# A decoder step with retention, RWKV-7 and product-key experts: the last gathered tile's sums stay in PSUM, and the first tile's output projection stands beside the second projection group

## The chip, the core and the metric

The kernel runs on one core of a Trainium2 chip. The metric is the device time of one execution in microseconds. The engines are named as in the profile: PE (TensorE: matmuls and transposes), DVE (VectorE), ACT (ScalarE), POOL (GpSimd), and SP, whose queue issues most of the DMAs. Each engine takes its instructions in the order in which they stand in its own list, and each DMA queue likewise.

## What is computed

One layer for 1024 prompt tokens and 64 sample tokens, width 1024, all in float32. Cut to the main line:

```
xn   = rmsnorm(h) * g
proj = xn @ w_in                          # 2048 retention + 1792 RWKV columns
out  = concat(retention(proj), rwkv7(proj)) @ w_out
h    = h + out
xn   = rmsnorm(h) * g2                    # PEER: 128 x 128 experts, 8 heads, top 16 each
q    = xn @ wq ; scores against two key sets ; top-k of top-k -> 128 experts per token
y    = sum_k gelu(xn . u[e_k]) * softmax_k * v[e_k]
h    = h + y
gate = sigmoid(rmsnorm(h) * g3 @ ple_gate)
h    = h + gate * (p @ ple_proj)
out  = rmsnorm(h) * g4
```

The recurrent states are outputs too. The two parts that the change touches are `h = h + out` for the first 128 tokens, and `h = h + y` for one tile of 128 tokens.

## The kernel before

The tokens are nine tiles: 0 to 7 are the prompt's, 128 tokens each, and 8 holds the 64 sample tokens.

**Projection.** `group_a` multiplies by `w_in` in three groups of tiles, `A0` = 0 and 1, `A1` = 2 and 3 (group two), `A2` = 4 to 8 (group three). Each streams all of `w_in` from HBM, splits every weight in a high and a low part, and uses three matmuls for one (L332, L333, L335). `a_ret` makes the retention columns (`pret` in PSUM), `a_rw` the RWKV columns (`prw`).

**Mixers.** `mixers(t)` does retention and RWKV for tile t. Tile 0's runs interleaved with groups one and two; its output row `od0` goes to HBM in two halves (L522, L994). The others follow group three in `group_b`.

**Rows.** `c_rows(t)` is the output projection of a tile: it loads x (L594) and `od` (L599), transposes (L604), multiplies by `w_out`, streamed in 16 pieces (L620, L621), adds (L624), stores `hd` (the residual stream, L625), norms, and stores `xd` (the experts' input, L639). In before, tile 0's call stands in `build` behind group two, and every step of it is followed by one step of group three (L1487).

**Experts.** Five tiles fetch their experts' rows one by one. `early_query` loads `xd` (L1196) and the query weights (L1213), multiplies (L1220), and picks the experts. `gather` then makes 128 steps over `u` (64 for tile 8): POOL issues an indirect DMA that brings one expert's row per token (L1146), and DVE multiplies it by x and sums (L1160); then as many steps over `v`, where DVE adds the weighted row onto `gacc` (L1172 the first, L1174 the others). `gacc` is one tile of two PSUM banks with a single buffer, which holds first x (L1154) and then the sums, so the gathers of tiles 0, 1, 8 (`E0`, in `early`) and 2, 3 (`G1`) follow each other. At the end of a gather ACT copies the sums to SBUF (L1178) and stores them in HBM as `yd` (L1179). Tiles 4 to 7 (`G2`) go through all 16384 experts as dense matmuls (`dense_fused`, `dense_stored`), with `gates` ahead of that for their routing weights; tiles 2 and 3 gather beside it.

**Last stage.** `ple` takes the tiles in the order 0, 1, 8, 4, 5, 6, 7, 2, 3. For each it loads `hd`, adds the experts' sums (a load of `yd`, L1424, and an add, L1425; the dense tiles' by transposes, L1430 and L1431), norms and transposes (L317, L326), then for each half of the columns 24 matmuls with the gate's weights (`ppg`), a sigmoid (L1440, L1441), 6 matmuls with the projection (`ppp`), L1444 and L1445, and at last the norm and the store of the output (L1448 to L1454).

**What sets the order.** The program is recorded with generators that yield after each small step; `build` and `interleave` decide which generator is asked next. A scheduler of the framework then fixes each engine's list from that, with priorities in the order of recording and a timing model of its own. So moving one call moves instructions on every engine.

Of the kernel before, what the change touches and what calls it, by code (L numbers as in the profile page):

```python
# [14 lines left out]
OP = mybir.AluOpType  # L15
# [166 lines left out]
E0 = [0, 1, 8]  # L182
G1 = [2, 3]
# [7 lines left out]
IB = 2  # L191
# [4 lines left out]
G2 = [4, 5, 6, 7]  # L196
# [21 lines left out]
class K:  # L218
# [917 lines left out]
    def gather(self, gp, t, rows=("grow",), parts=1, acc=None):  # L1136


        nc, I = self.nc, self.I
        n = SIZE[t]  # L1140
        slot = lambda name, tag: gp.tile([128, D], F32, name=name, tag=tag, bufs=GBUF if len(rows) == 1 else 1 + (tag == "V"))
        home = lambda: acc.tile([128, 2, 512], F32, name="gacc", bufs=1).rearrange("p a b -> p (a b)")

        def fetch(src, j):
            g = slot("grow", rows[j % len(rows)])
            nc.gpsimd.indirect_dma_start(out=g, out_offset=None, in_=src,  # L1146
                                         in_offset=bass.IndirectOffsetOnAxis(ap=self.eid[t][:, j:j + 1], axis=0))
            return g

        x = slot("gx", rows[-1])  # L1150
        for k in range(0, 128, n):
            nc.sync.dma_start(x[k:k + n], self.xd[t][:n])
        xs, x = x, home()
        nc.scalar.activation(x, xs, AF.Copy)  # L1154
        hv = gp.tile([128, parts, 128], F32, name="hv")[:, :, :n]
        cs = [slice(i * D // parts, (i + 1) * D // parts) for i in range(parts)]
        for j in range(n):
            g = fetch(I['pu'], j)
            for i, c in enumerate(cs):
                nc.vector.scalar_tensor_tensor(g[:, c], g[:, c], 1.0, x[:, c], op0=OP.mult, op1=OP.mult, accum_out=hv[:, i, j:j + 1])  # L1160
            yield j
        ac = gp.tile([128, 128], F32, name="ac")[:, :n]
        for i in range(1, parts):
            nc.vector.tensor_tensor(hv[:, 0], hv[:, 0], hv[:, i], op=OP.add)
        nc.scalar.activation(ac, hv[:, 0], AF.Gelu)
        nc.vector.tensor_tensor(ac, ac, self.gsm[t], op=OP.mult)
        y = home()
        for j in range(n):
            g = fetch(I['pv'], j)
            for c in cs:  # L1170
                if j == 0:
                    nc.vector.tensor_scalar(y[:, c], g[:, c], ac[:, 0:1], None, op0=OP.mult)  # L1172
                else:
                    nc.vector.scalar_tensor_tensor(y[:, c], g[:, c], ac[:, j:j + 1], y[:, c], op0=OP.mult, op1=OP.add)  # L1174
            if j < n - 1:
                yield j
        ys, y = y, slot("gy", rows[-1])
        nc.scalar.activation(y, ys, AF.Copy)  # L1178
        nc.scalar.dma_start(self.yd[t], y)  # L1179
        yield n  # L1180
# [225 lines left out]
    def ple(self, rp, tps, yT):  # L1406
        nc, I, O = self.nc, self.I, self.O
# [3 lines left out]
        for i, t in enumerate(E0 + G2 + G1):  # L1411
            tp = tps[i % 2]
            n = SIZE[t]
# [4 lines left out]
            self.split(pth[:, :, :n], ptl[:, :, :n], pt[:, :, :n])  # L1418
            h = tps[0].tile([128, D], F32, name="ph", bufs=3)
            nc.sync.dma_start(h[:n], self.hd[t][:n])  # L1420
            if t not in G2:
                for k in range(0, 128, n):
                    y = tp.tile([128, D], F32, name="py", tag="njunk")
                    nc.sync.dma_start(y[:n], self.yd[t][k:k + n])  # L1424
                    nc.vector.tensor_tensor(h[:n], h[:n], y[:n], op=OP.add)  # L1425
            else:
                o = self.off[t]
                p = self.pst.tile([128, 2, 512], F32, name="pyt").rearrange("p c (a b) -> p (c a) b", b=128)
                for d in range(8):
                    nc.tensor.transpose(p[:n, d, :], yT[:, d, o:o + n], self.c("ident"))  # L1430
                nc.vector.tensor_tensor(h[:n].rearrange("p (a b) -> p a b", b=128), h[:n].rearrange("p (a b) -> p a b", b=128), p[:n], op=OP.add)  # L1431
# [24 lines left out]
    def build(self):  # L1456
        PS = bass.MemoryType.PSUM
        run = lambda g: [None for _ in g]
        sb = lambda name, es, **kw: self.pool(name, es=es, reuse_waits="tile", **kw)
        with self.es:  # L1460
            self.setup()
            em, ee, eg, et, ew, ex, ep, e0, e1, e2 = (ExitStack() for _ in range(10))
# [10 lines left out]
            a = self.group_a(pools, A0, "b", mixes)  # L1473
            while next(a) != "rw":
                pass
            m = mix[0]
            self.interleave(m, 1, a, IA)
            a = self.group_a(pools, A1, "b")
            self.interleave(m, IB, a, 1)
            e1.close()  # L1480
            e0.close()
            self.ep0 = ep0 = sb("early", ee, side="right")
# [1 line left out]
            early = self.behind(self.early(ep0), PE_)  # L1484
            co = self.co = sb("co", ew, side="right")
            a = self.group_a(self.a_pool(e2, "2"), A2, "b")
            for _ in self.c_rows(co, E0[0]):  # L1487
                next(a, None)
            for _ in a:
                for _ in range(IE):  # L1490
                    next(early, None)
# [52 lines left out]
            with ExitStack() as e:  # L1544
# [9 lines left out]
                for i, t in enumerate(G2 + [None]):  # L1554
                    tk = self.topk(tp, t) if t is not None else iter(())
                    while True:
                        a, b = next(tk, "end"), next(gate, "end")
# [43 lines left out]
```

## Time and profile before

| | us |
|---|---|
| three timed runs | 3719.7, 3698.1, 3711.76 (median 3711.76) |
| the profiled execution | 3716.76 |
| its span, from the first to the last instruction | 3714.7 |

The profile's tables are read so. A line `L1174 DVE ... x571 | 731.9, 1282 | ...` is a group of instructions: how many, their busy time in us, the mean of one in ns, the idle time of the engine ahead of them and what ended it. A windows row gives, for a stretch of time, its length, the busy time (and number) of each engine, the clock that TensorE was granted (1.00 is full), the share of time in which the DMA engines were busy, and their rate. A row of the chain of waits is a start, a duration and what the end of the program was waiting for then.

The gathers' landmarks, from the tile view of `gacc`: the first tile's x is copied in at 447.7 us, the last tile's at 2980.9; the first sums are copied out at 1151.4 and the last at 3676.2.

### The profile page before, as it was taken

How to read it: one execution, taken by the hardware profiler on the slowest of the kernel's cores; microseconds unless marked ns; L12 is line 12 of the kernel's file. 1: busy time of each engine (PE TensorE's matmuls, PEld its weight loads, DVE VectorE, ACT ScalarE, POOL GpSimd, SP SyncE). 2: the span in 40 equal slices, each digit the busy share in tenths (PEclk: the TensorE clock that was granted, in tenths of full speed). 3: DMA queues.
4: the chain of work that ended last, by engine and by line, in shares of the span. 5: the costliest groups of instructions: out<-in, count | busy, mean ns of one | idle time of the engine just before them, and what ended most of it. 6: DMA issues, size and time to landing. Idle time of an engine off the chain costs nothing. (4 is left out here: it accounts for less than half of the span.)

```text
span 3714.7 us, 52379 instructions
## 1 busy us (share of the span) xinstructions
PE 3304.0 (89%) x17749; PEld 2745.7 (74%) x17749; DVE 2846.8 (77%) x5655; ACT 1216.7 (33%) x2260; POOL 2338.1 (63%) x2068
## 2 busy tenths in 40 slices
PE   7799995868869978897999999999999998899996
PEld 7698994645747866675887878887888876677774
DVE  5544578878796698877997989766777777877886
ACT  4232220111112111112334877863332333333322
POOL 5354276455454455555468877768888878887752
PEclk9799995667868567788999999999999999999998
DMA  7266588889867888889679988999999999999974
GB/s 254 84 207 207 190 276 290 275 276 326 290 218 278 299 274 280 287 287 328 212 253 320 327 291 291 341 344 348 342 340 346 332 357 366 370 361 360 330 270 157
DMA packets 423846, 1075.74 MB, mean 290 GB/s; under 512 B 46299, under 2 KB 143321, under 8 KB 418906
## 3 DMA queue, kind: packets, MB, share of 16 engines
q0 software_dynamic: 165888, 604.05, 46.1%
q1 hardware_dynamic: 202814, 377.55, 30.4%
q10 hardware_dynamic: 54876, 90.79, 6.6%
q8 instruction: 141, 2.31, 0.2%
q14 instruction: 127, 1.04, 0.1%
HBM read 981.46 MB, written 90.70 MB: 289 GB/s over the span
## 5 line engine op out<-in xcount | busy, mean ns | idle before, releaser
L1146 POOL DMA_INDIRECT grow<-in_pv,eid x576 | 567.1, 985 | 476.8 <-DVE gacc L1174 249.6
L1146 POOL DMA_INDIRECT grow<-in_pu,eid x576 | 560.9, 974 | 403.5 <-DVE grow L1160 222.1
L1160 DVE SCALAR_TENSOR_TENSOR grow<-grow,gacc 128x1024 f32<-128x1024 f32 x576 | 692.2, 1213 | 138.0 <-DMA grow<-in_pu,eid 123.2
L1174 DVE SCALAR_TENSOR_TENSOR gacc<-grow,ac,gacc 128x1024 f32<-128x1024 f32 x571 | 731.9, 1282 | 54.9 <-DMA grow<-in_pv,eid 46.9
L1329 PE MATMUL py<-ah,vh 128*128 128x512 f32 x1024 | 406.0, 397 | 31.5 <-ACT vh L303 28.6
L332 PE MATMUL ph<-cx,uh 128*128 128x512 f32 x1024 | 406.6, 397 | 11.9 <-DVE al L305 7.5
L1330 PE MATMUL py<-al,vh 128*128 128x512 f32 x1024 | 404.5, 395 | 3.1 <-DVE al L305 3.1
L333 PE MATMUL ph<-cx,uh 128*128 128x512 f32 x1024 | 405.5, 396 | 0.0
L307 POOL TENSOR_TENSOR vl<-vraw,vh 128x640 fp32r<-128x640 f32 (+1 forms) x224 | 325.4, 1458 | 39.3 <-ACT vh L303 29.5
L307 POOL TENSOR_TENSOR ul<-uraw,uh 128x1024 fp32r<-128x1024 f32 x128 | 307.8, 2404 | 59.4 <-ACT uh L303 30.5
L1332 PE MATMUL py<-ah,vl 128*128 128x512 f32 x1024 | 271.2, 396 | 6.9 <-POOL vl L307 6.8
L335 PE MATMUL ph<-cx,ul 128*128 128x512 f32 x1024 | 268.3, 398 | 2.3 <-POOL ul L307 2.3
L1329 PEld LDWEIGHTS py<-ah,vh 128*128 128x128 f32 x1024 | 194.7, 190 | 83.1 <-ACT vh L303 37.4
L303 ACT ACTIVATE vh<-vraw 128x640 fp32r<-128x640 f32 (+1 forms) x224 | 154.4, 692 | 266.9 <-DMA vraw<-in_pvd 89.6
L332 PEld LDWEIGHTS ph<-cx,uh 128*128 128x128 f32 x1024 | 195.0, 190 | 52.7 <-DVE al L305 7.9
L1332 PEld LDWEIGHTS py<-ah,vl 128*128 128x128 f32 x1024 | 191.4, 189 | 56.0 <-POOL vl L307 15.4
L1336 DVE TENSOR_TENSOR yT<-yT,py 128x512 f32<-128x512 f32 x216 | 147.6, 685 | 105.7 <-PE py L1332 86.1
L1330 PEld LDWEIGHTS py<-al,vh 128*128 128x128 f32 x1024 | 195.0, 190 | 45.1 <-DVE al L305 4.8
L333 PEld LDWEIGHTS ph<-cx,uh 128*128 128x128 f32 x1024 | 194.8, 190 | 38.4
L335 PEld LDWEIGHTS ph<-cx,ul 128*128 128x128 f32 x1024 | 191.6, 190 | 41.5 <-POOL ul L307 4.0
L303 ACT ACTIVATE uh<-uraw 128x1024 fp32r<-128x1024 f32 x128 | 135.4, 1058 | 149.5 <-DMA uraw<-in_puT 95.3
L1273 DVE TENSOR_TENSOR oh<-csta,pit 128x1024 f32<-128x1024 f32 x128 | 153.7, 1213 | 28.9 <-PE pwt L1278 15.9
(401 smaller groups left out, 7305.9 us busy)
## 6 DMA issues: line engine op xcount, KB each, us to landing
uraw<-in_puT SPq DMA_DIRECT2D x128, 512.0 KB
vraw<-in_pvd SPq DMA_DIRECT2D x128, 320.0 KB
cw<-in_w_out SPq DMA_DIRECT2D x128, 256.0 KB
wd<-wst ACTq DMA_DIRECT2D x28, 1024.0 KB
wt<-wd SPq DMA_DIRECT2D x64, 448.0 KB
wraw<-in_w_ret SPq DMA_DIRECT2D x48, 512.0 KB
ewq<-in_wq SPq DMA_DIRECT2D x48, 512.0 KB
vraw<-in_pvd SPq DMA_DIRECT2D x96, 256.0 KB
```

The costliest lines, as they stand in the source:

```text
L303: nc.scalar.activation(hi, src, AF.Copy)
L307: nc.gpsimd.tensor_tensor(lo, src, hi.bitcast(F32), op=OP.subtract)
L332: mm(out, lh(k), rh(k), start=first and k == 0, stop=False)
L333: mm(out, *((ll(k), rh(k)) if right else (lh(k), rl(k))), start=False, stop=False)
L335: mm(out, *((lh(k), rl(k)) if right else (ll(k), rh(k))), start=False, stop=last and k == nk - 1)
L1146: nc.gpsimd.indirect_dma_start(out=g, out_offset=None, in_=src, in_offset=bass.IndirectOffsetOnAxis(ap=self.eid[t][:, j:j + 1], axis=0))
L1160: nc.vector.scalar_tensor_tensor(g[:, c], g[:, c], 1.0, x[:, c], op0=OP.mult, op1=OP.mult, accum_out=hv[:, i, j:j + 1])
L1174: nc.vector.scalar_tensor_tensor(y[:, c], g[:, c], ac[:, j:j + 1], y[:, c], op0=OP.mult, op1=OP.add)
L1273: nc.vector.tensor_tensor(oh, io, p[:, 0:2, s + b:s + b + 4, None].to_broadcast([128, 2, 4, 128]), op=OP.is_equal)
L1329: nc.tensor.matmul(p, vh[:, b, :], ah, start=b == 0, stop=False)
L1330: nc.tensor.matmul(p, vh[:, b, :], al, start=False, stop=False)
L1332: nc.tensor.matmul(p, vl[:, b, :], ah, start=False, stop=b == nb - 1)
```

## The change

The first edit ends the gather of the last tile, `G1[-1]` = 3, without the copy, the store and the slot for them. The sums stay in `gacc`, and `ple` adds them from there. The other gathered tiles go through HBM as before.

The second edit takes the call `c_rows(co, 0)` from its place behind group two and puts it behind tile 0's mixer in the generator `first`, which `interleave` runs beside group two: `IB` = 2 steps of it for one of the group. It gets buffers of its own, the pool `co0`, which closes with group two's pools. Group three is then recorded with the early work alone.

```diff
@@ gather
+        if t == G1[-1]:
+            self.sums = y
+            yield n
+            return
         ys, y = y, slot("gy", rows[-1])
         nc.scalar.activation(y, ys, AF.Copy)
         nc.scalar.dma_start(self.yd[t], y)
@@ ple
-            if t not in G2:
+            if t == G1[-1]:
+                nc.vector.tensor_tensor(h[:n], h[:n], self.sums, op=OP.add)
+            elif t not in G2:
                 for k in range(0, 128, n):
                     y = tp.tile([128, D], F32, name="py", tag="njunk")
                     nc.sync.dma_start(y[:n], self.yd[t][k:k + n])
@@ build
             a = self.group_a(pools, A1, "b")
-            self.interleave(m, IB, a, 1)
+            co0 = sb("co0", e1, side="right")
+
+            def first():
+                yield from m
+                yield from self.c_rows(co0, E0[0])
+
+            self.interleave(first(), IB, a, 1)
             e1.close()
             e0.close()
...
             a = self.group_a(self.a_pool(e2, "2"), A2, "b")
-            for _ in self.c_rows(co, E0[0]):
-                next(a, None)
             for _ in a:
                 for _ in range(IE):
                     next(early, None)
```

Behind the first edit the lines of the changed kernel have higher numbers: by 4 from `gather` on, by 6 behind the add in `ple`, by 10 at the end.

Three places in the engines' lists show the move. First, SP's queue in the second half of group two. Before: the group's last weights (L534) between the first loads of group three (L375, L357), and tile 0's projection (L594, L599, L620) behind all of them.

```order
L375 DMA wraw<-in_w_ret 128x1024
L534 DMA wraw<-in_w_rw 128x1024 x2
L375 DMA wraw<-in_w_ret 128x1024 x2
L357 DMA x<-in_x 128x1024 x2
L534 DMA wraw<-in_w_rw 128x1024
L375 DMA wraw<-in_w_ret 128x1024
L534 DMA wraw<-in_w_rw 128x1024 x2
L357 DMA x<-in_x 64x1024
L534 DMA wraw<-in_w_rw 128x1024
L594 DMA ch<-in_x 128x1024
L599 DMA cot<-od_92 128x512 x2
L620 DMA cw<-in_w_out 128x512 x2
```

Now, in the same half of the group, SP's list reads:

```order
L534 DMA wraw<-in_w_rw 128x1024 x7
L599 DMA cot<-od_92 128x512
L620 DMA cw<-in_w_out 128x512 x3
L534 DMA wraw<-in_w_rw 128x1024 x2
L620 DMA cw<-in_w_out 128x512 x2
L534 DMA wraw<-in_w_rw 128x1024
L620 DMA cw<-in_w_out 128x512 x2
L534 DMA wraw<-in_w_rw 128x1024
L620 DMA cw<-in_w_out 128x512 x3
L534 DMA wraw<-in_w_rw 128x1024
```

The pieces of `w_out` stand between the group's last seven weights, behind a load of `od0` that waits for tile 0's mixer, and group three's loads have moved behind them.

Second, SP's queue where tile 0's query begins (L1196 loads its `xd`, L1213 its weights). Before, that is deep in group three, behind the sample states of the mixers (L433):

```order
L433 DMA sr<-in_s_ret 64x512
L391 DMA rope<-in_rope 128x256 x2
L1196 DMA exn<-xd_83 128x1024
L1213 DMA ewq<-in_wq 128x1024 x3
L391 DMA rope<-in_rope 128x256
```

Now it stands at the group's head (L1200, L1215 and L1217 are the former L1196, L1211 and L1213):

```order
L244 DMA row_norm_mix<-in_rows 128x1024
L375 DMA wraw<-in_w_ret 128x1024 x2
L357 DMA x<-in_x 128x1024 x2
L391 DMA rope<-in_rope 128x256 x3
L375 DMA wraw<-in_w_ret 128x1024 x3
L357 DMA x<-in_x 128x1024 x2
L1200 DMA exn<-xd_83 128x1024
L1215 DMA ekT<-in_keysT 128x128
L1217 DMA ewq<-in_wq 128x1024
```

The query has moved ahead of most of the group's own loads.

Third, the end of DVE's list, from the last-but-one tile (2) on. Before, the last gather steps (L1174) stand behind tile 2's output (L1453), and tile 3's add (L1425) behind them:

```order
L1441 TENSOR_SCALAR psg<-psg 128x512
L1174 SCALAR_TENSOR_TENSOR gacc<-grow,ac,gacc 128x1024
L1444 TENSOR_TENSOR psg<-psg,ppp 128x512
L1174 SCALAR_TENSOR_TENSOR gacc<-grow,ac,gacc 128x1024
L1445 TENSOR_TENSOR ph<-ph,psg 128x512
L1174 SCALAR_TENSOR_TENSOR gacc<-grow,ac,gacc 128x1024 x2
L1453 SCALAR_TENSOR_TENSOR fin<-ph,frs,row_norm_final 128x512 x2
L1174 SCALAR_TENSOR_TENSOR gacc<-grow,ac,gacc 128x1024 x3
L1425 TENSOR_TENSOR ph<-ph,py 128x1024
L317 SCALAR_TENSOR_TENSOR njunk<-ph,nrs,row_ple_norm 128x1024
```

Now (L1426 is the new add, L1447, L1450, L1451 and L1459 the former L1441, L1444, L1445 and L1453) the same end of DVE's list is:

```order
L1174 SCALAR_TENSOR_TENSOR gacc<-grow,ac,gacc 128x1024
L1426 TENSOR_TENSOR ph<-ph,gacc 128x1024
L1447 TENSOR_SCALAR psg<-psg 128x512
L1459 SCALAR_TENSOR_TENSOR fin<-ph,frs,row_norm_final 128x512 x2
L1450 TENSOR_TENSOR psg<-psg,ppp 128x512
L317 SCALAR_TENSOR_TENSOR njunk<-ph,nrs,row_ple_norm 128x1024
L1451 TENSOR_TENSOR ph<-ph,psg 128x512
L1447 TENSOR_SCALAR psg<-psg 128x512
```

The last gather step and tile 3's add stand ahead of tile 2's first sigmoid (the upper L1447), and tile 3's norm (L317) between tile 2's halves.

## The prediction

> **What bounds the kernel now.** I read the page first, then the stages, then the end.
>
> ```profile
> span 3714.7 us, 52379 instructions
> PE 3304.0 (89%) x17749; PEld 2745.7 (74%) x17749; DVE 2846.8 (77%) x5655; ACT 1216.7 (33%) x2260; POOL 2338.1 (63%) x2068
> L1160 DVE SCALAR_TENSOR_TENSOR grow<-grow,gacc 128x1024 f32<-128x1024 f32 x576 | 692.2, 1213 | 138.0 <-DMA grow<-in_pu,eid 123.2
> L1154 ACT ACTIVATE gacc<-gx x5: 1009/1029/1122, 447.7 to 2980.9; 128x1024 f32<-128x1024 f32 x5
> ```
>
> No engine is full over the whole span. Two strands run beside each other. One is the matrix work on PE. The other is the gather: 1152 DVE steps (576 of L1160 and 576 of L1172 and L1174) in one PSUM tile `gacc`, so the five tiles follow each other. It begins at 447.7 us (the tile view's row of L1154) and, as the chain below shows, ends at 3676.2, close to the end of everything. Busy time of each engine in eight stages, from one answer of the windows view (columns: window, its length, PE, weight loads, DVE, ACT, POOL, granted clock, DMA share, GB/s):
>
> ```profile
> 253.00:303.00 50.00, 39.38 (x293) 37.72 (x291) 30.24 (x50) 20.13 (x31) 30.61 (x25) 0.90 0.74 255
> 303.00:577.00 274.00, 258.38 (x2010) 249.35 (x2009) 163.76 (x466) 66.53 (x146) 136.42 (x147) 0.97 0.71 237
> 577.00:1197.00 620.00, 484.58 (x2740) 365.44 (x2741) 501.95 (x943) 92.59 (x208) 311.13 (x309) 0.70 0.82 279
> 1740.00:1960.00 220.00, 216.62 (x1211) 187.99 (x1212) 207.68 (x938) 69.93 (x110) 134.85 (x107) 1.00 0.74 246
> 2400.00:3000.00 600.00, 592.51 (x2704) 493.01 (x2703) 445.12 (x613) 232.29 (x388) 490.56 (x394) 0.99 0.96 341
> 3000.00:3530.00 530.00, 488.42 (x2050) 385.98 (x2048) 426.81 (x697) 195.69 (x321) 421.61 (x352) 0.98 1.00 359
> 3530.00:3715.00 185.00, 142.32 (x636) 112.18 (x636) 140.15 (x170) 41.90 (x79) 73.77 (x85) 0.89 0.63 213
> ```
>
> The third projection group (303 to 577) and the first part of the dense stage (2400 to 3000) are PE's; from 3000 to 3530 the DMA engines are full as well. A gather step there lies beside other work. In the last window PE is busy for only 142 of 185 us, and the chain of waits says why:
>
> ```profile
> 3542.66 1.24 DVE ph L1425
> ...
> 3674.90 1.30 DVE gacc L1174
> 3676.22 1.03 ACT gy L1178
> 3677.28 2.63 DMA yd<-gy
> 3679.96 3.32 DMA py<-yd
> 3683.31 1.24 DVE ph L1425
> ...
> 3688.09 1.94 PE ntr L326 x8
> ...
> 3706.05 0.49 PE ppp L335 x2
> ...
> 3710.28 1.30 DVEq L1597
> ```
>
> The last tile's gather ends at 3676.2, its sums go to HBM and back, and only then does that tile's last stage run, alone. PE's own rows for the last three tiles (the end of each half of a tile is the ppp row):
>
> ```profile
> 3650.92 0.63 PE L335 MATMUL ppp<-pgb,ptl 128*128 128x512 f32 x2
> 3657.73 0.62 PE L335 MATMUL ppp<-pgb,ptl 128*128 128x512 f32 x2
> 3664.53 0.61 PE L335 MATMUL ppp<-pgb,ptl 128*128 128x512 f32 x2
> 3688.09 1.94 PE L326 MATMUL ntr<-csta,njunk 128*128 128x128 f32 x8 [22.94 <-DVE njunk L317]
> ```
>
> PE waited 22.94 us for the last tile. A half of a tile costs 3657.73 - 3650.92 = 6.8 us when PE is fed.
>
> **The change part by part. (1) The sums stay in PSUM.** Removed: the copy L1178 (1.03 us), its store (2.63) and its load (3.32); with the gaps between them the add moves from 3683.31 to 3676.2, 7.1 us. The add itself reads PSUM in place of SBUF; I cost that at nothing. What is late next is the gather itself, and that is moved by the other part.
>
> **(2) The gather's lead.** Counted in DVE's order of before, 1102 gather steps stand ahead of the second L1425 (the one at 3542.66); in the change's order 1113 do, 11 more. From there to the first-half sigmoid of tile 2 it is 40 steps in before and 39 in the change, so DVE carries the same load per tile, but it finishes the gather one tile earlier: the new add stands just ahead of that L1441, which in before ran here:
>
> ```profile
> 3657.66 0.43 DVE L1441 TENSOR_SCALAR psg<-psg 128x512 f32<-128x512 f32 x1 [0.62 <-ACT psg L1440]
> ```
>
> So tile 3's sums are ready while PE still works on tile 2, and tile 3's transposes follow PE's 3664.53 + 0.61 = 3665.1 directly. From there: transposes about 1 us, two halves at 6.8, so PE ends near 3679.8. Behind the last matmul the trace shows 3714.7 - 3706.5 = 8.2 us of sums, square, norm and store, which stay. New end 3688.0 at an unchanged start of the stage: **-26.7 us**. The 7.1 us of part 1 are inside it, not beside it. Without the lead they are all there is.
>
> **(3) The projection of tile 0 moved into group two.** What it issues: two loads of `od0`, one of x, 16 quarter-megabyte loads of W_out and two rows on SP's queue; 8 transposes and 32 matmuls on PE; the copies, sums and norm of one tile on ACT, DVE and POOL; two stores. The same instructions, some 50 us earlier. What it needs, and when it ran (rows of the timeline, of the window of L621 alone, of PE's waits from 253 to 311, of the tile view of `ewq`, and of the page's list of DMAs):
>
> ```profile
> 250.84 0.33 ACTq L994 DMA_DIRECT2D od<-hnx  x1
> ...
> 303.08 0.33 SPq L594 DMA_DIRECT2D ch<-in_x  x1
> ...
> 303.00:353.00 50.00, 15.54 (x32) 5.29 (x32) 0.97 0.61 187
> ...
> PE prw L332 <- ACT rb L552: 4.2, 1, 4.2
> ...
> 365.52 0.33 SPq L1196 DMA_DIRECT2D exn<-xd  x1
> L1213 SPq DMA_DIRECT2D ewq<-in_wq x16: 327/328/468, 365.9 to 421.1; - x16
> ...
> cw<-in_w_out SPq DMA_DIRECT2D x128, 256.0 KB
> ewq<-in_wq SPq DMA_DIRECT2D x48, 512.0 KB
> ```
>
> Tile 0's mixed rows are stored at 250.84, while group two still runs to 303. The projection there costs PE 15.54 us (the window of L621 alone), and before it lay in a stage where PE had 258 of 274 us. In 253 to 303 PE was idle for 50 - 39.38 = 10.6 us, one wait of them 4.2 us long for ACT. If the matmuls fill all of that, the two groups end 10.6 us earlier; if the 16 x 256 KB = 4.2 MB are not hidden on the DMA engines, which moved 255 GB/s there against 359 in the busiest stage, they cost 4.2 MB / 359 GB/s = 11.7 us. All six rows of PE's waits there name ACT, DVE or POOL (the longest is quoted) and none a load, so the filled end is the nearer one, and I take half the idle time: **-5 us** (ends -10.6 and +11.7).
>
> The clock belongs here. The granted clock was 0.90 in this window, against 1.00 in 1740 to 1960. The Trainium skill's page "TensorE: Matmul & The Clock Gate", section "HAM oscillation — how this bites in real kernels", says that idle gaps of PE over about 3.4 us send it back to half clock. The 4.2 us wait is such a gap, and the lower grant fits it. By the rule this term would go to its end of -10.6, if the moved matmuls close that gap; and the rule speaks against the change at the next place, if a new gap opens there.
>
> That next place is the head of group three. Tile 0's query now begins there at once: counted in PE's order, about 25 matmuls of the group stand ahead of it in place of some 360. Its 16 loads of half a megabyte were spread over 365.9 to 421.1 among the group's matmuls. At worst all 8.4 MB stand exposed at 359 GB/s: +23.4 us; at best nothing. SP's queue has been rearranged so that the first of them go out behind the group's fourth row tile, and PE still has the group's matmuls between the heads: **+2 us**.
>
> **(4) The mixers.** From 577 to 1740 DVE is the busiest engine (501.95 of 620 us in the first part). Between the first state update of the mixers and the last projected tile, before has 349 gather steps in DVE's order and the change 341. Eight steps at 1.213 us are 9.7 us; had DVE been the chain throughout, all of that would be won, were the gather hidden, none; a new order may also lose as much: **-3 us** (ends -10 and +10). In the query, gate and dense stages the counts of the two orders differ by at most three steps. No change there.
>
> The sum: -26.7 - 5 + 2 - 3 = **-32.7 us**. The profiled execution took 3716.76 us, 2.1 more than its span, and that is 5.0 above the median of the three runs shown (3711.76). 3716.76 - 32.7 = 3684.1; as a median 3711.76 - 32.7 = 3679.1.
>
> **The rivals.** *The lead is eaten.* The gather gains 11 places in DVE's order, but its rows come late (L1160 waited 123.2 us for them, above), so it ends as close to the end as before, and only the copy and two transfers go: 3711.8 - 7.1 = 3704.7. For it: DMA is full from 3000 to 3530. Against: the steps are pinned in order between instructions of the same tiles, at the density of before. *More is won.* Group two's idle time is filled to the last and the mixers give all of 9.7 us: -26.7 - 10.6 - 9.7 = -47.0, so 3664.8. For it: DVE's share in the mixers. Against: part of DVE's time there is a wait for others. *The weights of the early work come late* (the other side): group two waits 11.7 us for W_out, group three's head 23.4 us for the query's weights, the mixers lose 10 through the order, and since tile 0's experts are then known late, the gather's lead is gone too. That is -7.1 + 45.1 = +38.0, so 3749.8, slower. It is slower than before from the point where 7.1 of those 45.1 us are exposed, and by more than a measurement can miss from 25.7. Against it: PE did not wait for a load in this stretch, and DMA had a quarter of its time left (0.74 and 0.71). *The change does nothing*: it would need the old place of the last add; the order shows another.
>
> **How the numbers follow.** Forecast 3679, its own range 3665 to 3693: 0.52. More is won, around 3665 or below: 0.13. The lead is eaten, around 3705: 0.22. Late weights, 3712 to 3750: 0.13. About 0.5% (18.6 us) is what a measurement of this kernel can tell from no change, so faster means below 3693.2 and slower above 3730.3. Faster takes the first two cases, 0.65; slower the upper half of the last, 0.07; the same has the rest, 0.28 (the eaten lead and the lower half). The range runs from 3658, the deeper case and a little under, to 3712, where the late weights begin; it leaves out most of that last case and some 5 in 100 below.
>
> **What would show it.** In the profile of the changed kernel: the last L1174 well ahead of PE's last tile, and no wait of PE over some 3 us ahead of the last ntr (step 2); no yd store for tile 3 (step 1); the exn load near 305 to 320 and the first L1154 near 390 to 400 in place of 447.7, with PE busier than 39.4 of the 50 us behind 253 (step 3); the dense stage beginning 0 to 15 us earlier (step 4). Wrong it would be if the dense stage begins later than before, or if PE waits at the head of group three for ewq.

## The result and the profile after

| | kernel before, us | changed kernel, us | ratio (95% interval) |
|---|---|---|---|
| first measurement, 9 runs each | 3707.65 | 3678.95 | 0.9925 (0.9902 to 0.9948) |
| second measurement, 29 and 12 runs | 3699.16 | 3683.89 | 0.9960 (0.9942 to 0.9978) |
| profiled execution | 3716.76 (span 3714.7) | 3683.49 (span 3681.7) | |

The change makes the kernel faster, by 28.7 us of the medians in the first measurement and by 15.3 us in the second. One of the nine runs of the kernel before took 4637.67 us and is left out of the ratio, which is estimated from the remaining runs, here and below, and so differs a little from the quotient of the two medians. Line numbers of the changed kernel are up to 10 higher than those of before, as the sections above say.

From the page of the changed kernel: the span, the engines' busy time, and the gather's first group.

```profile
span 3681.7 us, 52365 instructions
PE 3264.6 (89%) x17749; PEld 2715.2 (74%) x17749; DVE 2849.8 (77%) x5655; ACT 1217.2 (33%) x2259; POOL 2336.2 (63%) x2068
L1160 DVE SCALAR_TENSOR_TENSOR grow<-grow,gacc 128x1024 f32<-128x1024 f32 x576 | 691.2, 1213 | 144.9 <-DMA grow<-in_pu,eid 134.9
```

The work is the same. The end of the span looks different. The chain of waits of the changed kernel, from the end of tile 2 on (start, duration, what the end was waiting for):

```profile
3656.55 0.46 PE ppp L335 x2
3657.00 0.45 PE ntr L326 x4
3657.54 0.61 ACT pxh L303
...
3672.91 0.49 PE ppp L335 x2
3673.42 0.70 DVE psg L1450
```

From 3641 on no gather step and no transfer stands in it any more; ahead of that the chain goes through a load of `hd` (8.89 us from 3623.95). Tile 3's transposes (3657.00) follow tile 2's last matmul directly. The reason stands in DVE's timeline: the last gather step, tile 3's add from PSUM, and tile 3's norm are over before PE asks for them.

```profile
3647.69 1.28 DVE L1174 SCALAR_TENSOR_TENSOR gacc<-grow,ac,gacc 128x1024 f32<-128x1024 f32 x1
3649.00 1.22 DVE L1426 TENSOR_TENSOR ph<-ph,gacc 128x1024 f32<-128x1024 f32 x1
...
3652.60 1.29 DVE L317 SCALAR_TENSOR_TENSOR njunk<-ph,nrs,row_ple_norm 128x1024 f32<-128x1024 f32 x1
```

The windows of the changed kernel over the stretches that the prediction used:

```profile
253.00:303.00 50.00, 47.57 (x321) 39.49 (x320) 20.08 (x43) 15.96 (x24) 23.88 (x19) 1.00 0.88 286
303.00:577.00 274.00, 247.71 (x1971) 244.67 (x1969) 199.71 (x491) 70.78 (x149) 154.34 (x163) 0.96 0.75 249
577.00:1197.00 620.00, 459.94 (x2615) 344.85 (x2616) 499.23 (x930) 89.95 (x202) 301.56 (x303) 0.71 0.81 271
3530.00:3715.00 185.00, 134.21 (x612) 104.58 (x610) 121.91 (x155) 40.64 (x76) 61.52 (x71) 0.97 0.50 166
```

In the first row PE is busy for 47.6 us instead of 39.4, and the granted clock is 1.00 instead of 0.90: the moved projection fills group two's idle time, as hoped. The second row has 247.7 us of PE work where there were 258.4, but that is no loss by itself, since the moved projection has left this window. The price shows when the window ends with the group: group three's last transposes (L570) start at 573.6 before and at 584.0 now. From 253 to there, before and after:

```profile
253.00:573.60 320.60, 295.63 (x2294) 285.34 (x2292) 190.60 (x509) 86.65 (x176) 164.39 (x169) 0.97 0.72 239
```

```profile
253.00:584.00 331.00, 295.28 (x2289) 284.16 (x2288) 223.06 (x542) 87.21 (x175) 181.62 (x186) 0.96 0.78 257
```

PE does the same work (295.6 and 295.3 us) and stands idle for 35.7 us in place of 25.0. In the first 50 us it gains 8.2, behind them it loses 18.9.

### The profile page after: what moved, and what is told of

It reads as the page before. It is cut to its first block, busy times and chain, and to the rows that moved or that the text cites. A ratio compares the mean times of both kernels' runs of the same rounds, so it can differ in the third digit from the quotient of the medians.

```text
span 3681.7 us, 52365 instructions
## 1 busy us (share of the span) xinstructions
PE 3264.6 (89%) x17749; PEld 2715.2 (74%) x17749; DVE 2849.8 (77%) x5655; ACT 1217.2 (33%) x2259; POOL 2336.2 (63%) x2068
## 3 DMA queue, kind: packets, MB, share of 16 engines
q1 hardware_dynamic: 202670, 377.02, 30.9%
## 4 chain that ended last, share of the span: by engine, by line
PE 41%; DVE 20%; DMA 17%; issue 9%; POOL 8%; ACT 4%; ACTq 0%; SPq 0%; POOLq 0%; DVEq 0%
PE py L1333 5%; PE py L1336 5%; PE py L1334 5%; DVE grow L1160 4%; POOL grow L1146 4%; DVE gacc L1174 4%; PE ph L332 4%; PE ph L333 3%; PE ph L335 3%; DMA grow<-in_pu,eid 3%; DMA vraw<-in_pvd 2%; DMA grow<-in_pv,eid 2%; DMA gd<-geh 1%; PE epq L1224 1%; PE pwt L1282 1%
## 5 line engine op out<-in xcount | busy, mean ns | idle before, releaser
L1174 DVE SCALAR_TENSOR_TENSOR gacc<-grow,ac,gacc 128x1024 f32<-128x1024 f32 x571 | 731.8, 1282 | 52.2 <-DMA grow<-in_pv,eid 47.9
L1333 PE MATMUL py<-ah,vh 128*128 128x512 f32 x1024 | 406.0, 397 | 26.6 <-ACT vh L303 26.5
L1336 PE MATMUL py<-ah,vl 128*128 128x512 f32 x1024 | 274.2, 396 | 9.3 <-POOL vl L307 8.9
L1336 PEld LDWEIGHTS py<-ah,vl 128*128 128x128 f32 x1024 | 192.1, 189 | 58.4 <-POOL vl L307 17.2
L1277 DVE TENSOR_TENSOR oh<-csta,pit 128x1024 f32<-128x1024 f32 x128 | 153.3, 1213 | 28.7 <-ACT oh L1279 12.2
```

Source lines behind the costliest of these rows:

```text
L1277: nc.vector.tensor_tensor(oh, io, p[:, 0:2, s + b:s + b + 4, None].to_broadcast([128, 2, 4, 128]), op=OP.is_equal)
L1333: nc.tensor.matmul(p, vh[:, b, :], ah, start=b == 0, stop=False)
L1336: nc.tensor.matmul(p, vl[:, b, :], ah, start=False, stop=b == nb - 1)
```

## The experiments

Each was profiled once, and all but two were timed several times; the kernel before was timed beside them on the same chip. "Before's median" is that of the runs beside it. The kernels that change `co0` or the ring ran on other chips than the second measurement of the changed kernel.

**1. Which part gives the tail.** Three kernels: each edit alone, and both with the query held back.

The first edit alone (`e1_sums_only`):

```diff
-            co0 = sb("co0", e1, side="right")
-
-            def first():
-                yield from m
-                yield from self.c_rows(co0, E0[0])
-
-            self.interleave(first(), IB, a, 1)
+            self.interleave(m, IB, a, 1)
...
             a = self.group_a(self.a_pool(e2, "2"), A2, "b")
+            for _ in self.c_rows(co, E0[0]):
+                next(a, None)
```

> The first edit alone: tile 3's sums stay in PSUM, tile 0's projection stays behind group two. Theory 'lead' (the gather's eleven places ahead, which come from the moved projection, are what lets tile 3 follow tile 2 on PE): here there is no lead, so the first gather's x is copied in at about 448 us and the last gather step ends at about 3676 as before; only the copy, the store and the load go (7.1 us), PE still waits some 15 us ahead of the last tile's transposes, and the median is about 7 us below the kernel before. Rival 'the sums in PSUM free the end by themselves': last gather step near 3649, no wait ahead of the last tile, 25 to 29 us below the kernel before.

The second edit alone (`e2_proj_only`) has the copy, the store and the load of tile 3's sums again:

```diff
-        if t == G1[-1]:
-            self.sums = y
-            yield n
-            return
...
-            if t == G1[-1]:
-                nc.vector.tensor_tensor(h[:n], h[:n], self.sums, op=OP.add)
-            elif t not in G2:
+            if t not in G2:
```

> The second edit alone: tile 0's projection moves into group two, tile 3's sums go through HBM as before. Theory 'lead': the first x is copied in near 405 us and the gather ends near 3649, so its sums are back by about 3656 to 3658, when PE has just finished tile 2; PE waits 0 to 6 us ahead of the last tile's transposes, and the median is 22 to 29 us below the kernel before. Rival 'the two edits add up, each with a share of its own': about 22 below. Rival 'the sums edit does the work': no change (0 to 5 us below), last gather step near 3676.

Both edits, with ten steps of group three recorded ahead of the early work (`e3_query_held`):

```diff
             a = self.group_a(self.a_pool(e2, "2"), A2, "b")
+            for _ in range(10):
+                next(a, None)
```

> Both edits, but tile 0's query is held back: ten steps of group three are recorded ahead of the early work, as many as the projection took before. Theory 'lead': the projection still runs in group two, but the query begins where it did (first x copied in at about 440 to 450 us), so there is no lead; the gather ends near 3670 to 3676 and the median is 5 to 10 us below the kernel before. Rival 'the room in group two is what pays, not the lead': 20 to 29 us below, with the gather's end moved by as much. On the side: group three ends at 584.0 us in the changed kernel against 573.6 before; if the query at the group's head costs those 10 us, it ends here near 574, and if the moved projection does, near 584.

PE's wait ahead of the last tile's transposes, from the waits of 3640 to 3715, in the three kernels in this order (us in total, times, longest):

```profile
PE ntr L326 <- DVE njunk L317: 15.9, 1, 15.9
```

```profile
PE ntr L326 <- DVE njunk L317: 5.0, 1, 5.0
```

```profile
PE ntr L326 <- DVE njunk L317: 13.2, 1, 13.2
```

Before it was 22.9, in the changed kernel it is gone. With the query held back the gather starts later than in the changed kernel (434.5 in place of 404.6 us, the tile view of `gacc`):

```profile
L1154 ACT ACTIVATE gacc<-gx x5: 1017/1028/1037, 434.5 to 2960.9; 128x1024 f32<-128x1024 f32 x5
```

But the start is not what decides: a kernel of section 3 (`e5_in_group_three`) starts its gather at 435.2 and has the short tail all the same. What goes with the tail is the prediction's own count, the gather steps that stand ahead of the last stage's second add in DVE's order: 1102 in the kernel before and with the sums alone, 1104 with the query held back, 1113 in the changed kernel and with the projection alone, 1114 in `e5_in_group_three`.

A measure of the tail is the time from the last addition of the dense stage (L1336) to PE's last matmul, both inside one execution:

| kernel | last L1336 starts | PE ends | between | against before |
|---|---|---|---|---|
| before | 3529.8 | 3706.5 | 176.7 | |
| before, once more | 3517.6 | 3694.7 | 177.1 | +0.4 |
| sums in PSUM only | 3509.1 | 3679.2 | 170.1 | -6.6 |
| projection moved only | 3532.9 | 3688.9 | 156.0 | -20.7 |
| both, query held | 3520.8 | 3689.1 | 168.3 | -8.4 |
| changed kernel | 3524.4 | 3673.4 | 149.0 | -27.7 |
| changed kernel, once more | 3517.5 | 3667.7 | 150.2 | -26.5 |
| changed kernel, third profile | 3531.0 | 3681.4 | 150.4 | -26.3 |
| the changed kernel's lists (`e6_co0_left`, section 3) | 3528.2 | 3674.0 | 145.8 | -30.9 |

The last four rows have the same lists and lie between 145.8 and 150.4, so a single row is good to some 5 us. So the sums in PSUM are worth about what the two transfers and the copy cost (7.1 predicted, 6.6 here), the moved projection with its lead is worth 20.7, and with a lead of 2 places (third kernel) little more than the 7 us is left. The theory of the lead holds. The rival "the sums edit does the work" falls. The rival that the two edits add up, each with a share of its own, fits the tail as well (6.6 + 20.7 = 27.3).

Two expectations were missed on the way. With the sums alone the last gather step ended at 3655.9 and not near 3676, since that execution was 20.7 us earlier already at the last L1336. With the query held back group three ended at 581.0, so most of the 10 us that the group loses in the changed kernel are lost without the early query too.

The times of the whole kernels were less kind: sums only 3687.36 (0.9968, 0.9950 to 0.9985), projection only 3696.40 (0.9973, 0.9949 to 0.9996), query held 3699.81 (1.0004, 0.9980 to 1.0027), beside 3699.59 of the kernel before. The projection alone gained 20.7 us at the end and only about 10 in all (0.0027 x 3699.6); the third kernel gained 8.4 at the end and nothing in all. By these figures both lose about 10 us somewhere ahead of the tail, and both contain the moved projection; but each interval is some 17 us wide.

**2. What is the change and what is spread.** Both kernels once more, and the changed one timed again:

> The changed kernel once more, for the spread of its landmarks from one execution to the next. If the differences between the two profiles along the way (group three's end +10.4, the last pick +11.7, the first step of the dense stage -4.9) belong to the change, they come again within 3 us; if they are spread, they move by 5 to 12 us. The last gather step and the end of PE come again about 24 us apart by both.

> The kernel before once more, for the spread of its landmarks. If the changed kernel's group three ends 10 us later because of the change, this one ends it within 1 us of 573.6 again, while the first mixer update, the picks and the gates may move by up to 15 us from one execution to the next. From the last addition of the dense stage to PE's end it takes 176.7 us again, within 1.5.

> The changed kernel timed beside the kernel before in the same call as the two below, for a ratio on the same chip. 25 to 31 us below the kernel before, as the first measurement gave; if the two edits were additive by the single runs (12 and 3 us below) it would be 15 below.

`before_again` took 3705.0 us, `after_again` 3677.79, and the timed one 3683.89, 15.3 below the kernel before: not the 25 to 31 expected, but what the two edits' own medians add up to (12.2 and 3.2). Landmarks, all start times from the timelines. Left, three profiles whose lists are before's up to the end of the gather (before, once more, sums only); right, five whose lists are the changed kernel's up to the last stage (changed, once more, third, and two kernels of the sections below, `e4_dense_second` and `e6_co0_left`):

| landmark | like before: mean (single ones) | like the change: mean (single ones) | difference |
|---|---|---|---|
| group three's end (L570) | 573.8 (573.6, 572.6, 575.1) | 586.7 (584.0, 584.4, 592.3, 586.5, 586.3) | +12.9 |
| third state update of the mixers (L931) | 1036.0 (1039.0, 1033.4, 1035.7) | 1058.0 (1055.9, 1050.6, 1065.9, 1058.1, 1059.5) | +22.0 |
| last state update (L931) | 1670.8 (1679.5, 1669.5, 1663.5) | 1681.9 (1683.1, 1674.4, 1685.1, 1681.3, 1685.5) | +11.1 |
| last pick of the query (L1045) | 1896.5 (1905.3, 1894.8, 1889.5) | 1917.4 (1917.0, 1911.2, 1921.9, 1917.4, 1919.4) | +20.9 |
| last addition of the dense stage (L1336) | 3518.8 (3529.8, 3517.6, 3509.1) | 3524.5 (3524.4, 3517.5, 3531.0, 3521.3, 3528.2) | +5.7 |

The kernel with the projection moved only has the changed kernel's lists up to the gather's end too and is not in these means. Its landmarks are 585.1, 1058.1, 1687.4, 1923.9 and 3532.9; with it the last difference is +7.1, and the others move by at most 1.1.

Group three's end lies within 2.5 us in the three profiles on the left and within 8.3 on the right, and the two ranges are 8.9 us apart, so the delay there belongs to the change. Further on the same lists differ by up to 21 us from one execution to the next (3529.8 against 3509.1), most of it gathered between 577 and 1680. Of the first two profiles alone I would have read -5.4 at the dense stage's end; the means say +5.7, and neither is certain to better than some 10 us. What comes again in every one of the eight, and in the ninth, is group three's delay and the shorter stretch behind the last pick: from the last L1045 to the last L1336 it is 1619.6 to 1624.5 on the left and 1603.9 to 1609.1 on the right.

**3. Where group three loses 10 us.** The windows view from 303 to 320, before and after:

```profile
303.00:320.00 17.00, 13.48 (x101) 13.28 (x101) 9.99 (x17) 7.03 (x14) 6.38 (x10) 0.90 0.54 164
```

```profile
303.00:320.00 17.00, 4.91 (x23) 4.18 (x22) 9.73 (x17) 8.61 (x14) 10.31 (x10) 0.63 0.75 244
```

PE has almost stopped, and the granted clock falls to 0.63. PE's timeline of the changed kernel names the wait, which the kernel before doesn't have:

```profile
313.06 1.97 PE L326 MATMUL ntr<-csta,njunk 128*128 128x128 f32 x8 [9.79 <-DVE njunk L317]
```

These are the transposes of group three's first rows of x, behind their norm. The rows themselves are asked for much later than before. SP's timeline, before and then after (the last load of W_out stands just ahead of L633 there):

```profile
255.60 1.25 SPq L357 DMA_DIRECT2D x<-in_x  x2
```

```profile
286.15 1.54 SPq L633 DMA_DIRECT2D cgr<-in_rows  x2
...
295.44 8.69 SPq L357 DMA_DIRECT2D x<-in_x  x2
```

The rows were asked for at 255.6, now at 295.4, and the second one only some 8 us after the first. SP's waits from 285 to 320 and DVE's from 303 to 340 show what it stood for:

```profile
SPq L357 <- DMA xd<-ch: 7.9, 1, 7.9
```

```profile
DVE rb L540 <- DMA xd<-ch: 4.8, 1, 4.8
```

Both wait for the store of tile 0's normed rows, issued at 296.9 and landed 6.9 us later. DVE waits since its copy writes where `ch` lay. SP's load shares a completion counter with the store: in the trace the DMAs of SP and ACT signal eight semaphores in turn, the second load and the store have the same one, and the load went out at 303.80, when the store had landed (303.79).

SP's wait is not what PE stood for, though. The first row of x had landed at 302.5 by the counter's record in the trace, while PE's last matmul of group two ended only at 303.3. The norm's first step (L313, on ACT) began 6 us after the landing. ACT's timeline says why:

```profile
305.12 0.39 ACT L552 ACTIVATE rb<-prw 128x256 f32<-128x256 f32 x1 [4.54 <-DVE rb L540]
...
307.49 1.05 ACT L303 ACTIVATE wh<-wraw 128x1024 fp32r<-128x1024 f32 x1
308.44 1.05 ACT L313 ACTIVATE njunk<-x 128x1024 f32<-128x1024 f32 x1
```

In ACT's list the norm now stands behind group two's last copies (L552) and two splits of weights, and the copies waited for DVE's, which waited for the store. In the kernel before it stood in the middle of group two and ran at 269.71. From L313 to PE's transposes it takes another 4.6 us.

One kernel moves the pool `co0` and leaves every list as it is:

```diff
-            co0 = sb("co0", e1, side="right")
+            co0 = sb("co0", e0)
```

> The changed kernel with one word changed: the pool co0, in which tile 0's projection works, stands on the other side of SBUF (with the pools of tile 0's mixer, no longer above group two's). Every engine's list is the same, row for row. What differs is one wait: in the changed kernel DVE stands for 4.8 us (the row 'DVE rb L540 <- DMA xd<-ch' in the waits of 303 to 340), since a copy for group three's RWKV columns, recorded 200 us ahead of its use, is to write where co0's ch lay, and must wait until ch is stored; with co0 elsewhere it waits for a load of W_out that is long done. Theory 'the store holds up the change of groups': that wait goes, the waits of ACT for rb (4.5) and of POOL behind it (4.3) go with it, PE's idle time between 303 and 320 shrinks by 4 to 5 us and group three ends at 578 to 581 in place of 584; the end moves by 0 to 5 us, which the median can hardly tell. Rival 'the order alone does it': group three's x is asked for behind all of W_out on SP's queue, so PE waits for it as long as before, group three ends at 583 to 586.

DVE's wait for `xd` is gone, SP's is still there (7.6 us), PE's wait only falls from 9.8 to 8.6, and the clock stays low (0.62 from 303 to 320):

```profile
PE ntr L326 <- DVE njunk L317: 8.6, 1, 8.6
```

Group three ends at 586.3, as the rival had it. But ACT's list was held again, by another store: POOL waited for one of `fd`, DVE for POOL, and ACT for DVE.

```profile
302.98 0.61 POOL L557 TENSOR_TENSOR fdst<-rb 128x256 f32<-128x256 f32 x1 [2.92 <-DMA fd<-fdst]
```

```profile
306.67 0.39 ACT L552 ACTIVATE rb<-prw 128x256 f32<-128x256 f32 x1 [4.26 <-DVE fdst L558]
...
307.90 1.05 ACT L313 ACTIVATE njunk<-x 128x1024 f32<-128x1024 f32 x1
```

The first row had landed at 301.2 there. So the new order makes the gap, as the rival says, but by the place of the norm in ACT's list behind copies that wait for stores, and not by the rows' arrival. That a norm recorded further ahead would close the gap was not tried. The time was 3682.01 (8 runs) beside 3707.62, 0.9931 (0.9908 to 0.9954), between the changed kernel's two ratios.

The other way round, the projection was put back into group three, in one piece:

```diff
             a = self.group_a(self.a_pool(e2, "2"), A2, "b")
+            for _ in range(2):
+                next(a, None)
+            run(self.c_rows(co, E0[0]))
```

> Sums in PSUM, but tile 0's projection is recorded in group three again, in one piece behind the group's first two steps, in place of one step of it for each step of the group. In DVE's order the second add of the last stage has 1114 gather steps ahead of it, as the changed kernel's has 1113, and group three's first loads of x stand between group two's weights as in the kernel before. Theory 'lead': the tail is as short as the changed kernel's (about 27 us less from the dense stage's end to the end of PE), and group three is not held up at its head, so it ends at 574 to 580 in place of 584; in all 27 to 36 us below the kernel before. Rival 'the room in group two is what pays': PE's idle time there (some 10 us of 253 to 303) comes back, so 12 to 20 us below the kernel before.

The tail is as short as the changed kernel's (3532.9 to 3685.1, 152.2 us), so the lead does not need group two. But group three ended at 601.7, not at 574 to 580: PE's list now has the query's first transposes close behind the projection, and they wait for the projection's rows to come back from HBM, for 13.1 of the 28 us that the group ends later than before:

```profile
PE etr L1206 <- DMA exn<-xd: 13.1, 1, 13.1
```

The time was 3682.44 (0.9955, 0.9932 to 0.9978), as the changed kernel's 3683.89 beside it. The 15 us that group three lost more than the changed kernel (601.7 against 586.7) came through in part at most: the dense stage's last addition started at 3532.9 against a mean of 3524.5, 1.9 us above the latest of those five.

**4. The stall at the start of the last stage.** I took PE's stall there for some 11 us in both kernels and put a dense tile second. The rows have less: behind the last L1336 PE waits once for 7.0 us in the kernel before (6.3 in its second profile), and in the changed kernel for 4.3 us of the first 30, in pieces.

```diff
-        for i, t in enumerate(E0 + G2 + G1):
+        for i, t in enumerate(E0[:1] + G2[:1] + E0[1:] + G2[1:] + G1):
```

> The changed kernel with the last stage in the order 0, 4, 1, 8, 5, 6, 7, 2, 3 in place of 0, 1, 8, 4, 5, 6, 7, 2, 3. PE stands for 11 to 12 us at the start of that stage, where the tiles 0, 1 and 8 wait for their sums from HBM. If a dense tile, whose sums come from yT in SBUF, fills that time, the end is 8 to 11 us earlier than in the changed kernel. Rival 'the first tile alone sets that wait, or its hd load does, which a dense tile has too': within 2 us of the changed kernel.

PE's idle time in those 30 us fell from 4.3 to 0.3. From the dense stage's end to PE's end it took 148.4 us (3521.3 to 3669.7) against 145.8 to 150.4: no gain that the spread lets through, and the 8 to 11 us were not there to be won. The median was 3679.64 (0.9944, 0.9924 to 0.9965).

**5. Room on SP's queue.** `co0` on the other side, and a ring of six buffers for the projection's loads:

```diff
-                yield from self.c_rows(co0, E0[0])
+                yield from self.c_rows(co0, E0[0], 6)
```

> As the kernel before this one, and the ring in which W_out's pieces, od0 and the norm's rows are loaded has six buffers in place of four. In SP's list the last pieces of W_out then stand ahead of group two's last three weights, so the projection ends earlier, the xd store with it, and group three's x is asked for right behind the group's last weight. Theory 'the x loads of group three, late on SP's queue, open the gap at its head': PE's wait there (9.8 us) falls to 0 to 6 and group three ends at 573 to 579. Rival 'PE's time at the change of groups is set by group two's own last columns': group three ends as in the kernel before this one, within 1.5 us.

> The candidate with everything that has helped: sums in PSUM, the projection in group two with its pool on the other side and six buffers, and a dense tile second in the last stage. From the dense stage's end to PE's end 148 to 150 us, as with the reordered stage alone (148.4). If the head of group three is what is left of the cost of the move, and what it gives comes through to the end, 22 to 32 us below the kernel before; if the stretches behind it take it back, 16 to 22, as the reordered stage alone gave.

> The kernel of e7_left_ring6 once more. In its profile tile 0's head start grew to -32 us by the last mixer update, far more than the 2 us that group three's end had gained over e6_co0_left. If those 30 us belong to the new order, they come again within 10 us and the ratio to the kernel before is 0.988 to 0.993 again; if they are spread from one execution to the next, the last mixer update comes 0 to 10 us from the changed kernel's 1683.1 and the ratio is 0.992 to 0.996, that of the changed kernel.

In the first of the three PE's wait at group three's head falls to 7.3 us (from the waits of 303 to 340), and the norm's first step begins at 304.99 in place of 307.90:

```profile
PE ntr L326 <- DVE njunk L317: 7.3, 1, 7.3
```

Group three ends at 582.2, 581.7 and 579.2 in the three kernels, 4 to 7 us earlier than with four buffers and the pool on that side (586.3; 584.0 to 592.3 in all five profiles with four): less than the 573 to 579 hoped for. The first x is still asked for only at 293.0. The whole kernel gained far more than that:

| kernel | last state update of the mixers | time, us | before's median | ratio (95% interval) |
|---|---|---|---|---|
| six buffers | 1647.3 | 3665.83 | 3707.62 | 0.9908 (0.9879 to 0.9937) |
| six buffers, dense tile second | 1656.2 | 3671.53 | 3707.62 | 0.9906 (0.9879 to 0.9932) |
| six buffers, once more | 1656.3 | 3653.90 | 3697.13 | 0.9887 (0.9862 to 0.9912) |

With four buffers the last state update was at 1674.4 to 1685.5, 1681.9 in the mean; with six it is at 1653.3. Of the 28.6 us between them, 5.7 come from group three's earlier end (581.0 against 586.7), and 23 are won inside the mixers; the two ranges of the last state update do not touch (1656.3 and 1674.4). The tail is no shorter (155.2, 150.9 and 151.6 us). This version beats the kernel before clearly: the mean of its two ratios is 0.9898. It was not timed beside the changed kernel, whose two ratios were 0.9925 and 0.9960; the nearest is `e6_co0_left`, with the changed kernel's lists, 3682.01 us among the same runs as 3665.83 and 3671.53. The dense tile second gave nothing more (0.9906 beside 0.9908). What in the mixers is shorter is open. The ring of six changes the lists of all engines behind group three as well, since each step of the record moves the next, and no run took those moves apart.

## Why the prediction was right or wrong

The predicted 3679 met the first measurement (3678.95), and 3683.89 of the second lies within its own range of 3665 to 3693. That the first was met so closely is luck: the step forecast was -32.7 us from three runs with a median of 3711.76, and the measured steps were -28.7 and -15.3 from medians of 3707.65 and 3699.16. By its steps:

**(1) and (2), the sums and the lead: -26.7 predicted, -26.3 to -27.7 measured** in three profiles of the changed kernel and -30.9 in a fourth with the same lists, and -6.6 and -20.7 for the parts, which add up to 27.3. Right in size and in mechanism: the tail follows the places in DVE's order (1102 and 1104 without the lead, 1113 and 1114 with it). The add from PSUM took 1.22 us where the one from SBUF took 1.24, so to cost it at nothing was right. The statement that without the lead the 7.1 us are all there is was right too (-6.6 and -8.4 with no lead and with 2 places of it).

**(3) the projection in group two: -5 predicted, +2 for group three's head; group three ended 10.4 us later in the first pair, 12.9 in the mean.** This step failed. Half of it happened as written: PE's idle time from 253 to 303 fell from 10.6 to 2.4 us. What the step put at the query's weights (+2) came from elsewhere. It asked whether W_out is hidden and whether `ewq` comes in time, and it looked at SP's list around both; it did not ask what becomes of group three's first steps, although the list showed its x moved behind W_out. The rows were asked for 40 us later, and their norm moved on ACT from 269.7 to 308.4, behind group two's last copies and the stores that these wait for. That left PE without work for 9.8 us up to 313, and smaller gaps followed (in 303 to 320 it was busy for 4.9 of 17 us). The room of 8.2 us in group two was paid for by 18.9 us of idle time behind it. The end in which W_out is exposed (+11.7) has the right size for the wrong reason: for W_out itself PE waited 0.8 us.

The clock went as the Trainium skill's page "TensorE: Matmul & The Clock Gate", section "HAM oscillation — how this bites in real kernels", would have it at both places. With the 4.2 us wait closed the grant rose from 0.90 to 1.00; with a new wait of 9.79 us it fell to 0.63 in 303 to 320. The prediction's remark that the rule speaks against the change where a new gap opens was the better guide. The 3.4 us that the Trainium skill gives there are not a sharp limit in this trace, though. In the kernel before the clock was also halved behind a wait of 2.0 us that ended at 279.5:

```profile
279.80:283.10 3.30, 3.30 (x18) 3.30 (x17) 3.19 (x2) 0.39 (x1) 3.17 (x3) 0.50 0.82 276
```

So the 4.2 us wait accounts for 6.8 of the 10.2 us at half clock in 253 to 303 (266.1 to 272.9 and 279.8 to 283.2 in the trace's clock record), and not for all of the lower grant.

**(4) the mixers: -3 predicted, between -2 and +9 measured**, depending on the landmark (against group three's end the third state update is another 9 us late, the last one 2 us less late). No sign can be given, and the bounds of -10 and +10 were right. The reading that DVE is the busiest engine from 577 to 1740 holds only up to 1197; from 1197 to 1740 PE is busy for 458.5 us and DVE for 437.1. "No change in the query, gate and dense stages" was wrong: from the last pick to the dense stage's end the changed kernel needs 15 us less in the mean, in all profiles (1603.9 to 1609.1 against 1619.6 to 1624.5). DVE's wait for the softmax of tile 2's picks is one piece that the rows show, first before, then after, in the gates:

```profile
DVE sm L1116 <- ACT ex L1114: 11.9, 3, 5.9
```

```profile
DVE sm L1116 <- ACT ex L1114: 2.4, 3, 0.9
```

That this is the cause was not tried. The shorter stretch gave back most of what the earlier stages had lost, so that the sum of the errors is small: the part ahead of the tail was put at -6.0, and it is -5.4 in the first pair and +5.7 in the means. The sign that the prediction named for being wrong, a dense stage that begins later, came in the means: its first product with the routing weights (L1309 of the kernel before) starts 4.9 us earlier in the first pair and 3.4 us later in the means of the three and five profiles. The total lies in the range since the tail, its largest term, was right; the terms ahead of it were not.

**The rivals.** The lead was not eaten: the last gather step ends 27.2 us earlier (3649.0 against 3676.2). "Late weights" named the right place, group three's head, and the price of about 10 us, and had the wrong cause: it was the norm of x on ACT and no load of weights. "More is won" did not happen with this change; it did with six buffers.

## What to carry to other kernels

Measure a change at the end from one landmark to another inside one execution: there 7 and 20 us showed within 5 us, while the last L1336 spread by 20 with the same lists. When work is moved into a stage with idle time, look at each list that it passes, of queues and of engines, for the first step of the next stage that now stands behind it; here the room gained was lost where the next stage begins. A lead counted in places of an in-order list held at the end to some 4 us; the time gained in group two did not come through.

## What was not expected of the hardware

A load waited for a store with which it shares the completion counter: 7.9 us on SP for `xd`, and 7.6 with the store's source on the other side of SBUF. The store took 6.9 us to land while the DMA engines were 0.88 busy (296.9 to 303.8). A store of the same size, tile 3's sums in the kernel before, took 2.63 us near the end, where they were 0.51 busy (3677.3 to 3679.9). And the same lists spread by 21 us up to the dense stage's end (3509.1 to 3529.8), 16 of them already at the mixers' last state update (1663.5 to 1679.5) and 2.5 at group three's end. What makes an execution late there was not tried.
